# Recurrence part: the attention's output rows of both halves loaded at its beginning, into tiles that are written later

## The chip, the cores and the metric

The kernel runs on one core of one Trainium2 chip. The metric is the device time of one execution in microseconds (us), median of several runs. A core has a tensor engine for matmuls (PE, with PEld for its weight loads), a vector engine (DVE), a scalar engine (ACT), GpSimd (POOL) and a sync engine (SP); here SP only issues transfers between HBM and the on-chip memory (SBUF), in the order of its queue. ACT and POOL issue some as well. All transfers of a core run on the same 16 DMA engines.

## The reference, cut to what matters

One block of a hybrid model on 1024 tokens of width 1024, all in float32: a normalisation and an input projection, a recurrent branch (RWKV-7), a differential attention branch, a gated sum of both, an output projection, a mixture of 32 experts with two per token, and a gated extra embedding at the end. What matters here is the middle:

```python
o_rwkv = rwkv7_branch(p_rwkv, ...)            # [1024, 512], a scan over the tokens
o_diff = diff_attention_branch(p_diff, ...)   # [1024, 512]
mixed = (jax.nn.sigmoid(g_rwkv) * (o_rwkv @ w_branch_rwkv)
         + jax.nn.sigmoid(g_diff) * (o_diff @ w_branch_diff))
x = x + mixed @ w_out
```

## The kernel before

**Stages.** `build` emits: normalisation and input projection (`dense`, with the attention and the preparation of the recurrence, `w1`, spread among its matmuls); the recurrence `w2` with the branch projections as filler; the rest of the branch projections and the output projection with the router; the experts; the last stage. The attention writes its result to HBM, to `od` ([1024, 512]), one head at a time. The part that changes is the beginning of the recurrence part, some 700 us into the execution.

**The recurrence part.** `w2` runs over 8 chunks of 128 tokens. For each chunk `rwkv_gram` loads what `w1` has stored (tiles BK, AR, rows, rows2, LT; L360 to L367) and makes the Gram matrices `G` (PE L377 and L378 into the PSUM tile pG, then DVE L379); `rwkv_levels` loads the chunk's inverted blocks (Xd, L414), transposes them on DVE (L415) and inverts on PE (L422 to L449); `rwkv_step` and `rwkv_out` follow (L464 on). `rwkv_inv(1, ...)` inverts the blocks of chunks 4 to 7 on DVE alone: one load of 512 KB (`inv<-ld`, L390), then a copy (L396) and 30 pairs of multiply and add (L400, L402).

**The filler.** `fill` is a chain of generators. At each yield of `w2` a credit of 0.6 is added, and for every whole credit `fill` is advanced once. It begins with `branch_diff` for tokens 0 to 511 (half 0), then for tokens 512 to 1023 (half 1), then parts of `ple_proj` and of `branch` for the recurrent branch. `branch_diff` loads, for each of its four blocks of 128 tokens, the rows of `od` (256 KB, L779) into a tile `orow` with two buffers, transposes them with four PE instructions (L782, PSUM tile tpd, tag "a" with two buffers), and splits the transpose into a high part (ACT L76, odh) and a low part (DVE L77, odl), of which every matmul of the projection is made: `branch` (L755 to L769) loads eight slices of the weight (braw, split into bwh and bwl) and of the gate (bgt), makes 12 matmuls for each (L69 to L71, pbr), and DVE L766 writes the gated result to `md`.

**Tiles that play a part.** `md[i][k]` are four tiles of [128, 4, 512]: half i, output slices 4k to 4k+3. `md[1][1]` is first written by slices 4 to 7 of half 1. `K.orT[1]` is a pair of [128, 4, 512] tiles that `rwkv_out` fills from chunk 4 on (or1h by ACT L76, or1l by DVE L77). Both lie in memory that tiles of `w1` held before, so their first write waits for the last use of what lay there.

**What sets the order.** The text of the program gives each instruction a priority; a planner puts the instructions of each engine, and the transfers of SP's queue, in an order by that priority and by when its model thinks that an instruction's inputs and its memory are ready. So the order on a queue is not that of the text: the weight slices of `branch` (L755), for one, stand ahead of `ln_w` of `rwkv_setup` (L221). On the chip every queue then runs strictly in its order.

Of the kernel before, what the change touches and what calls it, by code (L numbers as in the profile page):

```python
# [22 lines left out]
F32 = mybir.dt.float32  # L23
# [12 lines left out]
W = 512  # L36
# [16 lines left out]
class Kern:  # L53
# [717 lines left out]
                nc.gpsimd.tensor_tensor(o, o, m, op=OP.add)  # L771
            yield

    def branch_diff(self, half, pool, md):
        nc = self.nc
        oT = [pool.tile([128, 4, 512], F32R, name=f"od{z}", tag=f"od{z}", bufs=1) for z in "hl"]
        for t in range(4):
            o = self.bp.tile([128, W], F32, name="orow", tag="orow", bufs=2)
            nc.sync.dma_start(o, self.od[half * 512 + t * 128:half * 512 + (t + 1) * 128, :])  # L779
            ps = self.ps.tile([128, 4, 128], F32, name="tpd", tag="a", bufs=2)  # L780
            for i in range(4):
                nc.tensor.transpose(ps[:, i, :], o[:, i * 128:(i + 1) * 128], self.ident)  # L782
            cs = slice(t * 128, t * 128 + 128)
            self.split(oT[0][:, :, cs], oT[1][:, :, cs], ps)
            yield
        yield from self.branch(1, half, oT, md)
# [528 lines left out]
def advance(g):  # L1315

    return next(g, StopIteration) is not StopIteration
# [14 lines left out]
def build(tc, A, out, dbg=None):  # L1332
    with ExitStack() as ctx:
        K = Kern(ctx, tc, A, out, dbg)
        nc = tc.nc
# [143 lines left out]
        md = [[K.mdtile(i).rearrange("p (k n) -> p k n", k=4) for _ in range(2)] for i in range(2)]  # L1479
        ob = [K.pool("ob1", ctx=B1, side="right")]  # L1480
# [8 lines left out]
        def from_turn(c, g):  # L1489
            while turn[0] < c:  # L1490
                yield
            yield from g


        ple = K.ple_proj(ob[0])
        fill = chain(K.branch_diff(0, ob[0], md[0]), K.branch_diff(1, ob[0], md[1]), islice(ple, 7),
                     from_turn(5, K.branch(0, 0, K.orT[0], md[0])), islice(ple, 4))
        K.credit = 0
        for c in w2():
# [94 lines left out]
```

## Time and profile before

| what | value |
|---|---|
| median of 3 runs | 1890.37 us (1888.12 to 1900.04) |
| the profiled execution | 1898.87 us, its span 1896.8 us |
| mean granted TensorE clock | 0.968 of full speed |
| PE, DVE, ACT, POOL busy | 95%, 71%, 45%, 15% of the span |
| DMA, mean over the span | 222 GB/s |

The span runs from the first to the last instruction; 2.07 us of the profiled execution lie outside it. Busy time is a mean over stages with different limits, so what one wait is worth has to be read where it stands. Matmuls are pipelined, so their bars overlap: a 128x512 matmul is listed with 0.39 us, and the next begins 0.23 us later.

### The profile page before, as it was taken

The numbers are of one execution on the slowest core, as the hardware profiler recorded it, in microseconds if no ns is written. First come the engines' busy times: TensorE is split into PE (matmuls) and PEld (weight loads), VectorE is DVE, ScalarE is ACT, GpSimd is POOL, SyncE is SP. The second block draws the span as 40 slices with busy tenths as digits, with TensorE's granted clock in tenths as the row PEclk, the third lists the DMA queues.
The fourth block names the chain that finished last, engine by engine and source line by source line (L and its number), as shares of the span: only waits on it lengthen the run. The fifth ranks groups of instructions, "written<-read, shape, count | busy, mean of one in ns | idle before, by whom it ended". The sixth has DMA issues, their size and how long they took to land. (4 is left out here: it accounts for less than half of the span.)

```text
span 1896.8 us, 28591 instructions
## 1 busy us (share of the span) xinstructions
PE 1794.4 (95%) x10864; PEld 1489.1 (79%) x10864; DVE 1342.8 (71%) x2580; ACT 858.1 (45%) x1241; POOL 275.7 (15%) x209
## 2 busy tenths in 40 slices
PE   6999999999998989999998996999999999999698
PEld 6999899898776776888876885888777777777487
DVE  6455867743777947766756668898878788888773
ACT  5244444421333322122223225777677777777431
POOL 0311201000222220010303001122111111110000
PEclk9999999999997998889998997999999999999799
DMA  6432242337576567444535557999999999999641
GB/s 219 129 117 78 79 134 79 100 112 251 192 254 228 186 206 247 141 137 158 172 110 191 176 180 254 370 367 376 328 344 356 369 357 357 348 348 354 261 176 45
DMA packets 241789, 421.39 MB, mean 222 GB/s; under 512 B 38769, under 2 KB 115697, under 8 KB 240754
## 3 DMA queue, kind: packets, MB, share of 16 engines
q1 hardware_dynamic: 194546, 346.12, 53.4%
q10 hardware_dynamic: 37888, 56.64, 8.2%
q0 software_dynamic: 9216, 16.80, 2.4%
q8 instruction: 86, 1.41, 0.3%
q14 instruction: 53, 0.43, 0.1%
HBM read 346.07 MB, written 90.18 MB: 230 GB/s over the span
## 5 line engine op out<-in xcount | busy, mean ns | idle before, releaser
L77 DVE TENSOR_TENSOR ewl<-ewp,ewh 128x2048 fp32r<-128x2048 f32 x108 | 245.6, 2286 | 38.1 <-ACT ewh L76 34.8
L69 PE MATMUL pj<-whi,hh 128*128 128x256 f32 x832 | 239.7, 288 | 0.0
L70 PE MATMUL pj<-wlo,hh 128*128 128x256 f32 x832 | 239.2, 288 | 0.3 <-DVE wlo L77 0.3
L71 PE MATMUL pj<-whi,hl 128*128 128x256 f32 x832 | 237.4, 286 | 0.0
L76 ACT ACTIVATE ewh<-ewp 128x2048 fp32r<-128x2048 f32 x108 | 204.5, 1912 | 18.3 <-PE pg L1163 8.5
L77 DVE TENSOR_TENSOR ewl<-md,ewh 128x2048 fp32r<-128x2048 f32 x84 | 191.2, 2286 | 28.0 <-ACT ewh L76 26.1
L69 PEld LDWEIGHTS pj<-whi,hh 128*128 128x128 f32 x832 | 159.2, 191 | 7.2 <-issue 6.6
L70 PEld LDWEIGHTS pj<-wlo,hh 128*128 128x128 f32 x832 | 159.2, 191 | 6.5 <-issue 5.3
L76 ACT ACTIVATE ewh<-md 128x2048 fp32r<-128x2048 f32 x84 | 159.3, 1910 | 9.6 <-PE pg L1163 4.2
L71 PEld LDWEIGHTS pj<-whi,hl 128*128 128x128 f32 x832 | 159.0, 191 | 2.6 <-issue 2.3
L1073 POOL DMA_INDIRECT xg<-h2d,ids x32 | 64.4, 2012 | 409.8 <-PE ptp L1063 390.5
L69 PE MATMUL pg<-hh,whi 128*128 128x512 f32 x256 | 105.7, 413 | 0.0
L70 PE MATMUL pg<-hl,whi 128*128 128x512 f32 x256 | 104.6, 409 | 0.0
L1163 PE MATMUL pu<-ewh,exh 128*128 128x512 f32 x256 | 103.5, 404 | 0.0
L71 PE MATMUL pg<-hh,wlo 128*128 128x512 f32 x256 | 103.1, 403 | 0.0
L1163 PE MATMUL pg<-ewh,exh 128*128 128x512 f32 x256 | 102.7, 401 | 0.0
L1163 PE MATMUL pg<-ewh,exl 128*128 128x512 f32 x256 | 102.3, 400 | 0.2 <-DVE exl L77 0.2
L1163 PE MATMUL pu<-ewh,exl 128*128 128x512 f32 x256 | 101.4, 396 | 0.0
L1116 PE MATMUL pey<-ewh,eal 128*128 128x512 f32 x256 | 97.7, 401 | 2.7 <-DVE eal L77 2.7
L1116 PE MATMUL pey<-ewh,eah 128*128 128x512 f32 x256 | 97.9, 402 | 1.4 <-ACT eah L76 1.4
L76 ACT ACTIVATE whi<-wraw 128x1024 fp32r<-128x1024 f32 x42 | 44.5, 1060 | 113.9 <-DMA wraw<-in_w_in_dram 56.4
L77 DVE TENSOR_TENSOR wlo<-wraw,whi 128x1024 fp32r<-128x1024 f32 x42 | 55.0, 1309 | 41.5 <-ACT whi L76 41.4
(457 smaller groups left out, 4262.6 us busy)
## 6 DMA issues: line engine op xcount, KB each, us to landing
ewp<-in_w_down_dram SPq DMA_DIRECT2D x42, 1024.0 KB, 7.7
ewp<-in_w_gate_dram SPq DMA_DIRECT2D x33, 1024.0 KB, 7.9
ewp<-in_w_up_dram SPq DMA_DIRECT2D x33, 1024.0 KB, 8.3
md<-in_w_up_dram SPq DMA_DIRECT2D x31, 1024.0 KB, 8.7
md<-in_w_gate_dram SPq DMA_DIRECT2D x31, 1024.0 KB, 7.6
md<-in_w_down_dram SPq DMA_DIRECT2D x22, 1024.0 KB, 7.4
wraw<-in_w_in_dram SPq DMA_DIRECT2D x42, 512.0 KB, 3.9
gd<-pjev ACTq DMA_DIRECT2D x32, 256.0 KB, 4.5
```

The lines of the kernel that those rows point to most:

```text
L69: mm(ps, lh, rh, start=start, stop=False)
L70: mm(ps, lh, rl, start=False, stop=False)
L71: mm(ps, ll, rh, start=False, stop=stop)
L76: a = nc.scalar.activation(hi, src, AF.Copy)
L77: b = nc.vector.tensor_tensor(lo, src, hi.bitcast(F32), op=OP.subtract)
L1073: self.lastx = self.nc.gpsimd.indirect_dma_start(out=xg, out_offset=None, in_=self.h2d, in_offset=bass.IndirectOffsetOnAxis(ap=tid, axis=0 ...
L1116: mm(self.pey[b], a[z][:, k + i, :], hi[:, i, half(b)], start=(k + i + z == 0), stop=False)
L1163: mm(P[i], x[z][:, k0 + j, :], hi[:, j, :], start=(k0 + j + z == 0), stop=False)
```

## The change

`branch_diff` gets one more argument, a tile `rows` of [128, 4, 512], and issues the four loads of its half into it at its start, followed by a yield. `build` makes both generators, gives half 0 the tile `md[1][1]` and half 1 the tile `K.orT[1][0]` seen as float32, and advances each once ahead of `w2`, so that all eight loads stand in the program ahead of the recurrence's own. The transposes read the new tiles. The tile `orow` of `branch_diff` is gone; `ple_proj` still has one of that tag, with 256 columns in place of 512.

```diff
-    def branch_diff(self, half, pool, md):
+    def branch_diff(self, half, pool, md, rows):
+
         nc = self.nc
+        for t in range(4):
+            r = half * 512 + t * 128
+            nc.sync.dma_start(rows[:, t, :], self.od[r:r + 128, :])
+        yield
         oT = [pool.tile([128, 4, 512], F32R, name=f"od{z}", tag=f"od{z}", bufs=1) for z in "hl"]
         for t in range(4):
-            o = self.bp.tile([128, W], F32, name="orow", tag="orow", bufs=2)
-            nc.sync.dma_start(o, self.od[half * 512 + t * 128:half * 512 + (t + 1) * 128, :])
             ps = self.ps.tile([128, 4, 128], F32, name="tpd", tag="a", bufs=2)
             for i in range(4):
-                nc.tensor.transpose(ps[:, i, :], o[:, i * 128:(i + 1) * 128], self.ident)
+                nc.tensor.transpose(ps[:, i, :], rows[:, t, i * 128:(i + 1) * 128], self.ident)
...
-        fill = chain(K.branch_diff(0, ob[0], md[0]), K.branch_diff(1, ob[0], md[1]), islice(ple, 7),
+        second = K.branch_diff(1, ob[0], md[1], K.orT[1][0].bitcast(F32))
+        first = K.branch_diff(0, ob[0], md[0], md[1][1])
+        advance(first)
+        advance(second)
+        fill = chain(first, second, islice(ple, 7),
                      from_turn(5, K.branch(0, 0, K.orT[0], md[0])), islice(ple, 4))
```

## Rows read from the trace of the kernel before

**Rows 1.** Page, part 1: busy us (share of the span) and instructions of each engine
```profile
PE 1794.4 (95%) x10864; PEld 1489.1 (79%) x10864; DVE 1342.8 (71%) x2580; ACT 858.1 (45%) x1241; POOL 275.7 (15%) x209
```

**Rows 2.** Waits of PE, 690 to 1160 us: who for whom, total, times, longest
```profile
PE tpd L782 <- DMA orow<-od: 6.7, 3, 2.7
```

**Rows 3.** Timeline of PE, half 0: start, duration, instruction, idle before and its releaser
```profile
703.44 0.60 PE L782 MATMUL tpd<-ident,orow 128*128 128x128 f32 x4
704.56 0.66 PE L782 MATMUL tpd<-ident,orow 128*128 128x128 f32 x4 [0.53 <-ACT pjev L743]
707.12 0.63 PE L782 MATMUL tpd<-ident,orow 128*128 128x128 f32 x4 [1.90 <-DMA orow<-od]
710.40 1.08 PE L782 MATMUL tpd<-ident,orow 128*128 128x128 f32 x4 [2.66 <-DMA orow<-od]
712.17 0.79 PE L69 MATMUL pbr<-odh,bwh 128*128 128x512 f32 x1 [0.69 <-ACT odh L76]
723.62 0.39 PE L71 MATMUL pbr<-odh,bwl 128*128 128x512 f32 x1
725.65 0.48 PE L377 MATMUL pG<-AR,BK 64*128 64x128 f32 x2 [1.65 <-DVE G L379]
```

**Rows 4.** Timeline of DVE around the same stretch
```profile
705.54 1.29 DVE L77 TENSOR_TENSOR odl<-tpd,odh 128x512 fp32r<-128x512 f32 x2 [0.72 <-ACT odh L76]
722.85 0.20 DVE L396 COPY inv<-inv 128x31 f32<-128x31 f32 x1 [4.65 <-DMA inv<-ld]
725.04 1.01 DVE L379 TENSOR_TENSOR G<-pG,gmask 128x384 f32<-128x384 f32 x2
```

**Rows 5.** Timeline of SP's queue: transfers as issued
```profile
672.36 22.80 SPq L348 DMA_DIRECT2D ld<-LT  x8
695.26 1.34 SPq L779 DMA_DIRECT2D orow<-od  x2
704.07 0.32 SPq L779 DMA_DIRECT2D orow<-od  x1
705.26 0.58 SPq L779 DMA_DIRECT2D orow<-od  x1
705.90 0.47 SPq L221 DMA_DIRECT2D ln_w<-in_rwkv_ln_w_dram  x1
710.13 0.52 SPq L390 DMA_DIRECT2D inv<-ld  x1
721.46 1.68 SPq L779 DMA_DIRECT2D orow<-od  x2
```

**Rows 6.** DMA issues, 706 to 724 us: count, KB each, median us to landing
```profile
DMA packets 3236, 5.85 MB, mean 325 GB/s; under 512 B 1283, under 2 KB 1795, under 8 KB 3235
inv<-ld SPq DMA_DIRECT2D x1, 512.0 KB, 12.6
ln_w<-in_rwkv_ln_w_dram SPq DMA_DIRECT2D x1, 256.0 KB, 6.2
```

**Rows 7.** Stretches: busy us by engine, PEclk, DMA share, GB/s
```profile
690.00:695.00 5.00, 5.00 (x28) 3.87 (x27) 1.29 (x2) 0.60 (x1) 0.00 (x0) 1.00 0.26 70
700.00:705.00 5.00, 4.47 (x24) 3.54 (x22) 1.46 (x3) 1.83 (x4) 2.34 (x4) 1.00 0.76 245
710.00:715.00 5.00, 3.91 (x10) 2.71 (x11) 0.69 (x1) 0.60 (x1) 0.00 (x0) 0.50 1.01 383
860.00:900.00 40.00, 40.00 (x453) 34.36 (x453) 26.15 (x65) 10.77 (x24) 2.56 (x2) 0.97 0.48 159
```

**Rows 8.** Half 1: timeline of PE, then of DVE
```profile
754.83 0.63 PE L782 MATMUL tpd<-ident,orow 128*128 128x128 f32 x4 [2.15 <-DMA orow<-od]
...
753.89 0.68 DVE L77 TENSOR_TENSOR odl<-tpd,odh 128x512 fp32r<-128x512 f32 x1
754.49 0.67 DVE L449 COPY XT<-pQ 64x512 f32<-64x512 f32 x1
```

**Rows 9.** First later writes to the second new tile
```profile
L76 ACT ACTIVATE or1h<-tpo x4: 590/597/597, 918.3 to 991.7; 128x512 fp32r<-128x512 f32 x4
```

## The prediction

> **What bounds the kernel now.** I read the page first: PE is busy for 95% of the span [rows 1], so a transfer matters only where PE stands still for it. The waits of PE from the beginning of the recurrence on come next: one row names the transfers that the change moves, 6.7 us in three waits, the longest 2.7 [rows 2]. That is all that the change aims at: 0.35% of 1898.87 us. The timelines then show where these waits stand and what would stop PE if they were gone.
>
> Half 0: the first two blocks of rows are in time. The third transpose waits 1.90 us and the fourth 2.66 us for their rows; then a split, and the first projection matmul starts at 712.17 [rows 3]. The cause is the two buffers of `orow`: the third and fourth loads go out only at 704.07 and 705.26, once transposes have freed a buffer [rows 5]. Half 1: the third transpose waits 2.15 us, until 754.83 [rows 8].
>
> The reader should also see the next gap. PE starts its last projection matmul at 723.62, stands still, and goes on at 725.65 with pG, said to wait for DVE's G [rows 3]. DVE is late because it is stuck on the copy at 722.85, which waited 4.65 us for the transfer `inv<-ld` [rows 4]. That transfer was issued at 710.13 [rows 5] and took 12.6 us to land, against 6.2 us for `ln_w`, issued at 705.90 on the same queue [rows 5, 6]. From 710 to 715 us the DMA engines are fully busy (share 1.01) [rows 7]. So this stretch is held by the DMA queue as a whole: a backlog that ends with `inv<-ld`.
>
> **The change, part by part.**
>
> *The waits of half 0.* With all rows there, what holds the third transpose is its PSUM buffer, free when the first low part is made. DVE makes two of them from 705.54 in 1.29 us [rows 4], so the first ends near 706.2 and the second near 706.8. The third transpose can start at 706.2 in place of 707.12, the fourth at 706.9 in place of 710.40. From the fourth transpose to the first matmul the trace takes 712.17 - 710.40 = 1.77 us, part of it at the low clock; I take 1.3 to 1.77, which gives 708.2 to 708.7. The projection starts 3.5 to 4.0 us earlier; I take 4.0.
>
> *What catches it.* The block from 712.17 to 725.65 then ends near 719.6 and PE again needs G. G comes after DVE's copy, and the copy after `inv<-ld`. So the gain in half 0 is not 4.0 us but what `inv<-ld` gains, unless that is more than 4.0. Everything turns on where the eight loads stand on SP's queue.
>
> *Placing A, ahead of the last `ld<-LT`.* The queue has eight of these, from 672.36 to 695.16 [rows 5], most of it waiting, and the DMA engines have room there: share 0.26 from 690 to 695 us [rows 7]. The old `orow` lies in memory that late steps of `w1` still use. The new tiles lie further to the edge of the region, by the order of allocation over tiles that the last preparations read first (their input rows). I think it likelier than not that the planner finds them free early. Then nothing of `od` is left in the crowded stretch: two issues of 0.32 and 0.58 us ahead of `ln_w` are gone [rows 5], and 2 x 0.26 = 0.52 MB at 325 GB/s (the mean of 706 to 724 us [rows 6]) are 1.6 us. `inv<-ld` lands 1.6 us (the bytes alone) to 2.5 us (both) earlier; I take 2.2. G, and PE with it, goes on at 723.45 in place of 725.65.
>
> *Placing B, behind the last `ld<-LT`,* where `orow` stands now (695.26). Then half 1's four loads, 1.05 MB, come ahead of the recurrence's loads: 1.05 MB / 325 GB/s = 3.2 us later. Some goes into the room that the DMA engines have from 700 to 705 us (share 0.76 [rows 7], so 0.24 x 5 = 1.2 us). `inv<-ld` then lands 2.0 to 3.2 us later and PE goes on at 727.7 to 728.9. The Trainium skill's page "DMA: Bandwidth & Descriptors", section "Queues, rings and completion order", says that each DMA engine consumes the descriptors of a ring in order. By that rule loads put in front delay all that follows, which speaks against this change; the landing times growing from 6.2 to 12.6 us agree with it, and it gives the case of placing B.
>
> *Half 1.* The third transpose needs the PSUM buffer of the first, whose low part DVE makes from 753.89 in 0.68 us, to 754.57 [rows 8]. It starts at 754.83 now, so 0.26 of the 2.15 us are to be had. Behind it PE needs DVE's copy of 754.49, which ends at 755.16 [rows 8]; that does not move with the loads of `od`. I take 0.3 us, bounds 0 and 2.15.
>
> *Issues and waits.* The same eight loads of 256 KB are issued, at 0.32 to 0.84 us each ([rows 5]; a pair takes 1.34 or 1.68). I cost their issue at nothing in A, where SP waits anyway; in B eight take 8 x 0.67 = 5.4 us and hold up the weight and gate slices, `ln_w` and the gram loads behind them, and the 3.2 us of transfer time run beside that. New waits: the loads wait for their tiles' former owners, and behind them on SP stand just these transfers. The other new edges cost nothing: `or1h` is first written at 918.3 [rows 9], over 150 us after the last transpose of half 1, and slices 4 to 7 of half 1 come after all transposes of half 0. The narrower `orow` of `ple_proj` saves memory and no time.
>
> *The clock.* PE is granted 0.50, the 1.2 GHz level, from 710 to 715 us after its stalls [rows 7]. PE is busy for 3.91 us of these five, so the half clock costs at most 3.91 / 2 = 2.0 us there. In A the gap at 704 to 710 shrinks but the one ahead of 723.45 grows to 3.8 us, so I count nothing either way.
>
> *Sum,* against the profiled execution of 1898.87 us (span 1896.8 and 2.07 outside): A -2.2 - 0.3 = -2.5 us, 1896.4. That execution lies 8.5 us above the median of 1890.37, so against the median the sum gives 1887.9. Once PE is past this place it is full (40.00 of 40 us from 860 to 900 [rows 7]), so what is won or lost here is carried to the end.
>
> **The rivals.**
>
> 1. *All waits go, and the gain passes.* If the loads go out early and `inv<-ld` lands by about 718.7 us, four earlier, PE loses nothing at pG: -4.0 in half 0, up to -2.15 in half 1, and up to 2.0 of low clock; I take -6.5 us, 1883.9, with -8.2 as the end. For it: the wait row's 6.7 us. Against it: the backlog of 325 GB/s would have to lose 1.3 MB, and 0.52 MB leave it.
> 2. *The transfers are only moved forward into the crowd (B).* The wait at the transposes turns into a longer wait at pG: PE reaches it at 719.6 and stands to 727.7 or later. +2.0 to +3.2, less 0.3 to 1 for half 1 and for the 0.5 MB that no longer run behind 721.46; about +2, 1892.4. It decides if the first load of `od` is issued behind the last `ld<-LT`. Slower, yet far inside 1%.
> 3. *The planner lays out another order.* The loads' earlier times can change the order of DVE and PE queues in all of the recurrence part. Nothing in the trace gives its size; the nearest rows are single waits of 2 to 3 us [rows 2, 3], so some tens of instructions would have to move badly or well to make 19 us. It can go both ways.
>
> **How the numbers follow.** Chances: A 0.45, rival 1 0.2, B 0.25, rival 3 0.1, half of it to each side. The forecast is A's: 1888.0. A's own range is 1885.7 (-2.5 and -2.15) to 1888.8 (-1.6 alone). The range has to take in rival 1 with its bounds, -8.2, so 1882.2; B's worst, +3.2, 1893.6; and that the three runs of before spread over 12 us, so that a median can lie some 3 us to either side. That gives 1878 to 1897; only rival 3 lies outside. A measurement of this kernel can tell about 1%, 19 us, from no change. A, B and rival 1 all lie within it: 0.90; rival 3 gives 0.05 to faster and 0.05 to slower.
>
> **What would show it.** Right: the row of PE waiting for `od` is gone or below 1 us; the first projection matmul of half 0 starts about 4 us sooner after the last input projection matmul; the wait at pG behind it is longer than 1.65 us; the third transpose of half 1 follows DVE's low part. A against B: on SP's queue the loads of `od` stand ahead of or behind the last `ld<-LT`, and `inv<-ld` lands earlier or later, counted from the last input projection matmul. Wrong: `inv<-ld` lands over 4 us earlier (rival 1), an `od` load holds SP for long on its tile's former owner, or the order of DVE's instructions after it is another (rival 3).

## The result, and the profile after

The changed kernel takes 1909.58 us in the median (1907.83 to 1914.94), the kernel before 1891.53 (1887.31 to 1900.04) beside it: 1.0095 times as long, 95% interval 1.0075 to 1.0115, some 18 us slower. The forecast was 1888.0 us with a range to 1897. The profiled execution of after took 1913.6 us, span 1911.5.

**Where the 18 us are.** Most of them not where the change was made. The last input projection matmul ends the part in front (703.2 us before, 701.9 after), the last transpose `tpo` the recurrence: 991.0 and 989.5, so the part that was edited takes 287.8 and 287.6 us in these two executions (others of the same two orders, further on, took 282.1 and 290.5). The difference of these two comes 450 us later, in the experts. One row for each kernel shows it; it gives the first and the last start of the transposes of the experts' inputs (tile view, PE's transposes of `xg`: count, shortest/median/longest ns, first to last start). Before, then after:

```profile
L1063 PE MATMUL ptp<-ident,xg x256: 270/272/475, 1161.2 to 1736.7; 128*128 128x128 f32 x128
```
```profile
L1066 PE MATMUL ptp<-ident,xg x256: 270/272/474, 1158.8 to 1749.7; 128*128 128x128 f32 x128
```

The same 256 transposes of the same length are spread over 575.5 us before and 590.9 after: 2.4 us ahead at the first, 13.0 behind at the last. What fills the stage shows in one stretch of it (window view, 1180 to 1730 us: length, then busy us of PE, weight loads, DVE, ACT and POOL with counts, granted clock, DMA share, GB/s), before and then after:

```profile
1180.00:1730.00 550.00, 534.51 (x2472) 426.78 (x2470) 465.85 (x353) 408.74 (x348) 97.29 (x57) 1.00 0.99 356
```
```profile
1180.00:1730.00 550.00, 528.47 (x2405) 421.75 (x2404) 455.48 (x346) 395.27 (x338) 98.56 (x56) 0.99 0.97 347
```

Before, the experts are bound by their weights: DMA share 0.99. After, the DMA engines have gaps (0.94 and 336 GB/s from 1450 us on), although not a byte and not a transfer was added here. The lower rate is the whole difference: by an estimate from these rows, 575.5 x 356 / 347 is 590 us. The waits of PE in that stretch name other instructions (who for whom: total us, times, longest). After:

```profile
PE pg L1166 <- ACT ewh L76: 9.2, 7, 2.0
PE pey L1119 <- ACT eah L76: 6.3, 9, 1.6
PE pey L1119 <- DVE eal L77: 4.7, 4, 1.6
```

Before, this was 17 short waits of `pg` for VectorE's low halves of the weights, and 2.7 and 0.7 us at `pey`; the row of the first:

```profile
PE pg L1165 <- DVE ewl L77: 11.6, 17, 0.8
```

After, PE waits longer, and for ScalarE. The rhythm tells why. ScalarE's silu `eac` comes once in each expert (timeline of ACT, lines of `eac` alone), before and then after:

```profile
1456.83 0.60 ACT L1198 ACTIVATE eac<-pg 128x512 f32<-128x512 f32 x1 [0.38 <-PE pg L1165]
1475.94 0.60 ACT L1198 ACTIVATE eac<-pg 128x512 f32<-128x512 f32 x1 [0.38 <-PE pg L1165]
1495.06 0.60 ACT L1198 ACTIVATE eac<-pg 128x512 f32<-128x512 f32 x1 [0.37 <-PE pg L1165]
1514.18 0.60 ACT L1198 ACTIVATE eac<-pg 128x512 f32<-128x512 f32 x1 [0.39 <-PE pg L1165]
```
```profile
1475.13 0.61 ACT L1201 ACTIVATE eac<-pg 128x512 f32<-128x512 f32 x1
1498.39 0.61 ACT L1201 ACTIVATE eac<-pg 128x512 f32<-128x512 f32 x1
1513.32 0.60 ACT L1201 ACTIVATE eac<-pg 128x512 f32<-128x512 f32 x1 [2.84 <-PE pg L1168]
1537.56 0.60 ACT L1201 ACTIVATE eac<-pg 128x512 f32<-128x512 f32 x1 [0.34 <-PE pg L1168]
```

Before, an expert takes 19.1 us, one like the other. After, 23.3, 14.9, 24.2. The programs show the same without any time: ScalarE's order in five experts in a row, the 14th to 18th (w a split of weights, x of inputs, a of activations, y the scaling of an output, S the silu):

```
before: wxwawxwwyywS wxwawwxwyywS wxwawwxwyywS wxwawwxwyywS wxwawwxwyywS
after:  wwaxwS wwywyxwaxwwyyxwS wwwaxwwyyxwS wxwawwwwxyywS wwaxwwwwyyxwS
```

The planner reaches one repeated pattern before and never settles after. In the expert stage the orders of ScalarE, VectorE and PE differ, SP's and GpSimd's don't. No line of the experts is in the diff.

**The edited place after.** SP's queue (timeline of SP) shows placing B; compare [rows 5]:

```profile
671.01 22.81 SPq L348 DMA_DIRECT2D ld<-LT  x8
696.67 1.77 SPq L779 DMA_DIRECT2D md<-od  x4
698.49 2.19 SPq L779 DMA_DIRECT2D or1h<-od  x4
700.72 0.43 SPq L755 DMA_DIRECT2D braw<-in_w_branch_diff_dram  x1
702.63 0.38 SPq L755 DMA_DIRECT2D braw<-in_w_branch_diff_dram  x1
703.60 0.93 SPq L1243 DMA_DIRECT2D orow<-in_p_dram  x2
709.69 0.46 SPq L221 DMA_DIRECT2D ln_w<-in_rwkv_ln_w_dram  x1
713.42 0.61 SPq L390 DMA_DIRECT2D inv<-ld  x1
```

All eight loads stand behind the last `ld<-LT` and in front of everything else; the first waited 2.5 us, released by these transfers. PE and VectorE in half 0 (timelines; compare [rows 3, 4]):

```profile
702.93 0.66 PE L785 MATMUL tpd<-ident,md 128*128 128x128 f32 x4 [0.25 <-ACT pjev L743]
709.92 1.97 PE L785 MATMUL tpd<-ident,md 128*128 128x128 f32 x8 [6.33 <-DVE odl L77]
712.58 0.79 PE L69 MATMUL pbr<-odh,bwh 128*128 128x512 f32 x1 [0.69 <-ACT odh L76]
...
706.91 0.69 DVE L77 TENSOR_TENSOR bwl<-braw,bwh 128x512 fp32r<-128x512 f32 x1 [15.60 <-ACT bwh L76]
708.50 0.69 DVE L77 TENSOR_TENSOR bwl<-braw,bwh 128x512 fp32r<-128x512 f32 x1 [0.90 <-ACT bwh L76]
709.18 1.28 DVE L77 TENSOR_TENSOR odl<-tpd,odh 128x512 fp32r<-128x512 f32 x2
```

The rows are there, and PE waits 6.33 us all the same: the third transpose needs the PSUM buffer that VectorE's `odl` frees, and VectorE stands at `bwl`, which is in front of `odl` on its queue in both kernels. `bwl` needs the first weight slices. These were issued at 696.69 before, behind two loads of rows, and are at 700.72 now, behind eight. The wait for transfers has become a wait for an engine that waits for transfers, and the projection starts 10.7 us after the last input projection matmul (9.0 before).

### The profile page after: what moved, and what is told of

It is laid out like the page before. It is cut to its first block, busy times and chain, and to the rows that moved or that the text cites. A ratio compares the mean times of both kernels' runs of the same rounds, so it can differ in the third digit from the quotient of the medians.

```text
span 1911.5 us, 28572 instructions
## 1 busy us (share of the span) xinstructions
PE 1796.7 (94%) x10864; PEld 1490.6 (78%) x10864; DVE 1347.0 (70%) x2580; ACT 856.3 (45%) x1241; POOL 278.2 (15%) x209
## 5 line engine op out<-in xcount | busy, mean ns | idle before, releaser
L1076 POOL DMA_INDIRECT xg<-h2d,ids x32 | 58.2, 1819 | 462.9 <-PE ptp L1066 443.3
L1166 PE MATMUL pg<-ewh,exh 128*128 128x512 f32 x256 | 107.0, 418 | 9.2 <-ACT ewh L76 9.2
```

Source lines behind the costliest of these rows:

```text
L1076: self.lastx = self.nc.gpsimd.indirect_dma_start(out=xg, out_offset=None, in_=self.h2d, in_offset=bass.IndirectOffsetOnAxis(ap=tid, axis=0 ...
L1166: mm(P[i], x[z][:, k0 + j, :], hi[:, j, :], start=(k0 + j + z == 0), stop=False)
```

## The experiments

All times are medians, ratios against the kernel before on the same chip. An order is held by edges between each instruction and the next on its engine; they fix the order in the engine's queue and add no wait on the chip. In the recurrence and the experts all programs here have the same compute instructions in the same sequence as recorded (e11 and e12: plus some), so one program's order can be given to another.

```diff
+        i0 = len(nc.cur_bb.bb.instructions)
         K.experts(raws, between)
...
+        pin_order(tc, nc.cur_bb.bb.instructions[i0:])
         K.overflow_loop()
...
+def pin_order(tc, ins):
...
+    for steps in json.loads(zlib.decompress(base64.b85decode(ORDER))):
...
+            tc.add_manual_dep(ins[at], ins[prev].name,
+                              mybir.DependencyInfo(C.NoSync, mybir.DependencyReason.DATA), reason="order")
```

**e1 and e2: the order in the expert stage, exchanged.** e1 is the change with the order of before there, e2 the kernel before with the order of after.

> The changed kernel, with the order of ACT's, DVE's and PE's instructions in the expert stage held to that of the kernel before; the early loads stay. Theory O (the planner's other order in the expert stage costs the time): the expert stage, first to last transpose of gathered rows, falls from 590.8 to about 575.4 us; the whole is 1889 us, 0.998 of before (the changed kernel began its experts 2.4 us earlier than before), range 1884 to 1894. Theory L (the early loads or their tiles cost it by themselves): stays near 1909 us, 1.009 of before.

> The kernel before, with the order of ACT's, DVE's and PE's instructions in the expert stage held to that of the changed kernel; its loads as before. Theory O: the expert stage rises from 575.4 to about 590.8 us, the whole to 1907 us, 1.008 of before, range 1902 to 1912. Theory L: no change, 1891 us.

e1: 1897.08 us, 1.0025 (1.0004 to 1.0046). e2: 1905.37, 1.0060 (1.0042 to 1.0079). Their expert stages take 575.3 and 587.4 us; the DMA share from 1180 to 1730 is 0.99 in e1, 0.96 in e2:

```profile
1180.00:1730.00 550.00, 533.77 (x2470) 426.29 (x2469) 466.04 (x355) 408.89 (x348) 97.25 (x57) 1.00 0.99 356
```
```profile
1180.00:1730.00 550.00, 528.29 (x2415) 421.10 (x2415) 456.52 (x346) 396.93 (x339) 99.61 (x57) 0.99 0.96 348
```

So the order of the experts, and none of the loads, makes 0.95% - 0.25% = 0.70% (13 us) by e1 and 0.60% (11 us) by e2. About 5 us (0.25%) stay in e1, more than expected.

**e3 and e4: one half alone.** In e3 half 0 is loaded early and half 1 the old way; in e4 the other way round. The edit of e3, against the change (without a tile `branch_diff` loads as before):

```diff
-        second = K.branch_diff(1, ob[0], md[1], K.orT[1][0].bitcast(F32))
+        second = K.branch_diff(1, ob[0], md[1])
         first = K.branch_diff(0, ob[0], md[0], md[1][1])
         advance(first)
-        advance(second)
```

> Half 0's four loads early into md[1][1], half 1's as before. The planner gives ACT the same order in the expert stage as before. Theory O: 1890 us, 1.000 of before, range 1885 to 1895, expert stage 575 us. Theory L: about half of the loss or more, 1900 us, since half of the loads are moved.

> Half 1's four loads early into or1h, half 0's as before. The planner's order in the expert stage falls into the steady pattern of the kernel before only at about the eighteenth expert, where before it does at the thirteenth and in the changed kernel at none. Theory O: between the two, the expert stage about 580 us, the whole 1896 us, 1.003 of before, range 1890 to 1902. Theory L: as with half 0, 1900 us.

e3: 1887.05, 0.9965 (0.9939 to 0.9991). e4: 1892.58, 1.0001 (0.9975 to 1.0026). Each came out 3 us better than its first number. With one half early, the planner finds the steady pattern (in e3 as early as before, in e4 some five experts later), and the stage takes 577.3 and 577.7 us. The loss of the experts needs both halves early. e3 lies below before with its whole interval; its profile, of the slowest of its ten executions, does not show why.

**e5 and e6: the 5 us of e1, by the queue or by VectorE.** Both hold the order of before in the experts. e5 takes both early calls away, so that half 0's loads stay where they are (the chain begins with them) and half 1's come when its turn comes; e6 keeps all loads and holds the first weight slices' splits behind the splits of the transposed rows.

```diff
-        advance(first)
-        advance(second)
```
```diff
-            self.split(wh, wl, raw)
+            self.split(wh, wl, raw, after=last if j == 0 and half == 0 else None)
```

> The changed kernel with the order of the kernel before held in the expert stage, as in e1; half 1's four loads are issued when the chain reaches half 1 and not at the beginning, half 0's four at the beginning as in the change. On SP's queue half 1's loads then stand behind the first two weight slices and gate slices, still ahead of the loads of p, of ln_w and of the recurrence's loads. Open are about 5 us that e1 (1897.1) keeps against the kernel before (1891.9) and that e3 (1887.1), with half 1 loaded the old way behind the recurrence's loads, does not show. Theory V (VectorE: the weight slices come late behind eight loads of rows, VectorE's split of them stands ahead of its split of the transposed rows, and PE waits 6.3 us for that): the weights are early again, the third transpose waits under 3 us for VectorE, the time is 1892 (1888 to 1894). Theory C (crowd: 1 MB more stands ahead of the recurrence's loads, and PE stops later at pG): nothing of that is changed, 1897 (1895 to 1900), and PE's wait at pG grows by what the transposes no longer wait. If the 5 us are neither, both kernels of V come out within 2 us of e1.

> The changed kernel with the order of the kernel before held in the expert stage, as in e1, and the queue order of all eight loads as in the change; in half 0 the splits of the first weight slices are held behind the splits of all four transposed blocks, on ScalarE and VectorE. Theory V (PE's 6.3 us at the third transpose come from VectorE standing at the weight slices' split): the wait of the transposes for VectorE falls to under 1.5 us, the first projection matmul starts under 9 us after the last input projection matmul (10.7 in the change), and the time is 1892 (1888 to 1894). Theory C (1 MB more ahead of the recurrence's loads): the transposes go early too, but what they win is lost again at pG, where the wait grows from 0.9 to 3 us and more; 1896 to 1898.

e5: 1900.65, 1.0049 (1.0031 to 1.0067). e6: 1883.87, 0.9954 (0.9938 to 0.9971), 9 us faster than before. Neither theory survives: both times lie outside the ranges of both. In e5 the wait for VectorE at the transposes fell from 6.3 to 2.2 us and the kernel got no faster; in e6 it fell to 3.4 only, on the queue order of the change, and the kernel got 13 us faster than e1. e6's edge had made the planner lay out the whole recurrence anew: it puts the gram matmuls and the projection side by side, and its recurrence takes 275.7 us (e1 290.5, e5 291.5). The window view of the whole recurrence, from the last input projection matmul to the last `tpo`, for before, after and e6:

```profile
703.20:991.00 287.80, 274.58 (x2481) 227.76 (x2480) 187.27 (x445) 65.17 (x131) 32.61 (x25) 0.92 0.51 160
```
```profile
701.90:989.50 287.60, 270.83 (x2482) 225.08 (x2480) 188.63 (x446) 65.82 (x132) 33.05 (x25) 0.93 0.51 162
```
```profile
701.00:976.70 275.70, 262.39 (x2481) 216.68 (x2480) 186.57 (x445) 65.73 (x132) 32.89 (x25) 0.96 0.53 169
```

PE stands still for 13.2, 16.8 and 13.3 us (length less busy), which does not tell e6 from before; the busy time differs by 12 us for the same matmuls, and the column that goes with it is the granted clock, 0.92, 0.93 and 0.96. I cut the recurrence of each kernel into stretches of 5 us and summed the idle time and, for the clock, busy time times one less the granted clock:

| kernel | recurrence | PE idle | lost by the clock | rest |
|---|---|---|---|---|
| before | 287.8 | 13.2 | 20.2 | 254.4 |
| before's recurrence in e2 | 282.1 | 12.4 | 14.9 | 254.8 |
| after | 287.6 | 16.8 | 16.0 | 254.8 |
| the same code in e1 | 290.5 | 15.7 | 19.6 | 255.2 |
| e3 | 284.8 | 13.9 | 15.7 | 255.2 |
| e4 | 282.4 | 13.4 | 14.0 | 255.0 |
| e5 | 291.5 | 15.2 | 20.4 | 255.9 |
| e6 | 275.7 | 13.3 | 8.2 | 254.2 |

The rest is the work at full clock, 254 to 256 us in all of them. The idle time moves by 4 us; what the clock takes moves by 12. The same code shows 20.2 and 14.9 in two executions (the change's 16.0 and 19.6), so that one profile of this stage says little to within 5 us. The idle time scatters less: 13.2 and 12.4 us for the code of before, 16.8 and 15.7 for the change's, 2.5 to 4.4 us more with the early loads.

**e7: ScalarE's order alone.** As e1, but with only ScalarE's order held.

> The changed kernel with the order of the kernel before held in the expert stage for ScalarE's instructions alone; VectorE's and PE's are laid out by the planner around it. If ScalarE's order (when the splits of the next weights stand ahead of or behind the splits of activations) is what costs the 12 to 13 us of the expert stage: time 1897 (1894 to 1900), expert stage about 576 us, PE waits for the weights' low halves in 17 waits again. If VectorE's or PE's order decides: 1903 to 1910, expert stage 583 to 591 us.

1930.00, 1.0201 (1.0172 to 1.0230), expert stage 609.1 us: outside both numbers, and worse than either whole order. ScalarE then has the order of before to the letter, and the planner's new order of VectorE and PE around it does not fit: PE waits 17.9 us for `ewh` at `pu`. Which engine's order costs can't be said one engine at a time.

**e8: no loads at all.** The transposes read the constant mask, so the rows' share of the result is missing; the order of before is held in the experts.

```diff
-            nc.sync.dma_start(rows[:, t, :], self.od[r:r + 128, :])
...
-                nc.tensor.transpose(ps[:, i, :], rows[:, t, i * 128:(i + 1) * 128], self.ident)
+                nc.tensor.transpose(ps[:, i, :], self.mask[:, i * 128:(i + 1) * 128], self.ident)
```

> The changed kernel with the order of the kernel before held in the expert stage, and without the eight loads of the attention's output rows: the transposes read a constant tile that is there from the start, so the attention's branch is left out of the result. This gives what no placement of these loads can beat. The prediction's first rival (all waits go and the gain passes on) has 6.5 us less than the kernel before: 1885 (1882 to 1888). If PE is stopped again at pG by the recurrence's own loads, whatever the rows do: the 1 MB of half 0 that is gone brings them at most 3 us forward, so 1888 to 1891, and a wait at pG of 2 us or more. If the recurrence takes up neither: 1892.

1958.45 us, but that total says nothing: with other values the router spreads the tokens otherwise, and a block of the overflow loop runs that the other kernels don't need (264 transposes of `xg` in place of 256). The recurrence lies in front of that. It takes 277.8 us, PE idle for 10.6, 14.9 lost by the clock. So without any of these loads the idle time is 13.2 - 10.6 = 2.6 us shorter than before (1.8 against e2's), about what the prediction's sum had (2.5), in an order of the recurrence that was not held. PE is stopped at `pG` all the same, now by the recurrence's own load, which is the expectation's second case (timeline of PE, the projection beginning at 710.60):

```profile
714.64 0.81 PE L377 MATMUL pG<-AR,BK 64*128 64x128 f32 x4 [3.46 <-DMA AR<-spAR]
```

**e9 and e10: layout against loads.** Now the orders of PE, ScalarE and VectorE are held from the recurrence to the experts' end: e9 is the kernel before with e6's order, e10 the change with the order of before.

> The kernel before, with its late loads into two buffers, and the order of PE's, ScalarE's and VectorE's instructions that the planner gave e6, from the recurrence's beginning to the end of the experts; SP's and GpSimd's orders are the planner's. In its profile e6 needs 275.7 us from the last input projection matmul to the end of the recurrence, the kernel before 287.8, the change 287.6. If the layout of the recurrence is what makes e6 fast and not its loads: 1884 (1880 to 1887), recurrence 274 to 279 us. If the early loads and the earlier splits make it: 1892 (1889 to 1895), recurrence 282 to 288 us, as the kernel before.

> The change with the order of PE's, ScalarE's and VectorE's instructions of the kernel before in the recurrence too, not only in the expert stage as in e1 (1897.1): what is left of the change is the loads. If the loads cost nothing and the 5 us of e1 are the layout of the recurrence: 1892 (1889 to 1895). If the loads themselves cost it (1 MB more ahead of the recurrence's loads, weight slices late): 1897 (1895 to 1900). If they bring what the prediction said, with the layout out of the way: 1889 or less.

e9: 1887.74, 0.9969 (0.9953 to 0.9985), between its two ranges; its recurrence takes 278.3 us, within the first, with 15.2 idle and 8.7 lost by the clock. With the late loads of before, two thirds of e6's gain (0.31 of 0.46%) come from the order alone; whether e6's loads make the rest is not settled, as the intervals overlap. e10: 1895.87, 1.0009 (0.9987 to 1.0032), which is from 2.5 us faster to 6.1 slower. By the time alone, the loads can't be told from nothing. The profile (of an execution of 1902.92 us, above the median) shows what they do in the order of before. PE waits 7.3 us for VectorE's `odl` at the third transpose. VectorE's copy of `inv` comes 24.3 us after the last input projection matmul (at 701.6), 19.7 before, and PE, waiting for the G behind it, goes on with `pG` 27.5 us after that matmul, 22.4 before (timelines of PE and DVE; compare [rows 3, 4]):

```profile
729.07 0.79 PE L377 MATMUL pG<-AR,BK 64*128 64x128 f32 x2 [3.13 <-DVE G L379]
725.92 0.20 DVE L396 COPY inv<-inv 128x31 f32<-128x31 f32 x1 [5.78 <-DMA inv<-ld]
```

Its recurrence takes 295.7 us: 17.0 idle (13.2 and 12.4 with the late loads), 24.4 lost by the clock, rest 254.3. So the loads hold PE up by some 4 us; how much of that reaches the time is not settled.

**e11: is a short stall paid twice?** The kernel before with 14 more matmuls at a place where PE stands still for 1.2 us; they repeat what was just written to their buffer.

```diff
+            if (c, h) == (2, 6):
+                for _ in range(7):
+                    self.again += [
+                        nc.tensor.matmul(ps[:, 0, :], BK[o:o + 64, pr, 0, :], AR[o:o + 64, pr, 1, :], start=True, stop=True),
+                        nc.tensor.matmul(ps[:, 1:3, :], BK[o:o + 64, pr, 1, :], AR[o:o + 64, pr, :, :], start=True, stop=True)]
...
+            if name == "PE" and n == 435:
+                order += again
```

> The kernel before with every engine's order as it is and 14 matmuls more: two of the gram matmuls of one head are repeated seven times, into the same buffer with the same values, right ahead of the place where PE stands still for 1.2 us about 93 us after the last input projection matmul (795 us in the profile of before). In that profile the granted clock is 0.72 to 0.85 in the 40 us from 80 to 120 us behind that matmul, 8.6 us lost by the clock, and 1.00 behind it. If a short stall is paid twice, once as itself and once by the clock that falls after it: PE is busy in that place, the clock stays at 1.00, and more work takes less time, 1885 to 1889. If the clock falls there for another reason: 1892 to 1893.

1886.22, 0.9962 (0.9942 to 0.9982): 7 us less for more work. The stall in the timeline of before, and the 80 us from 80 us behind the last input projection matmul on (window view), before and then e11:

```profile
795.97 0.48 PE L377 MATMUL pG<-AR,BK 64*128 64x128 f32 x2 [1.21 <-DVE G L379]
...
783.20:803.20 20.00, 18.80 (x210) 16.74 (x210) 12.27 (x25) 2.29 (x6) 1.30 (x2) 0.85 0.46 142
803.20:823.20 20.00, 20.00 (x102) 16.55 (x102) 10.29 (x28) 4.25 (x8) 2.55 (x2) 0.72 0.44 144
823.20:843.20 20.00, 20.00 (x248) 17.71 (x247) 12.79 (x33) 3.77 (x9) 0.00 (x0) 1.00 0.39 124
843.20:863.20 20.00, 19.02 (x124) 14.39 (x123) 11.83 (x25) 4.26 (x9) 2.55 (x2) 0.74 0.50 143
```
```profile
780.80:800.80 20.00, 20.00 (x238) 17.79 (x237) 12.36 (x24) 2.18 (x5) 2.04 (x2) 1.00 0.41 122
800.80:820.80 20.00, 20.00 (x168) 16.64 (x168) 14.62 (x33) 4.87 (x10) 2.58 (x2) 1.00 0.60 197
820.80:840.80 20.00, 19.81 (x219) 16.85 (x217) 13.71 (x37) 5.03 (x11) 2.55 (x2) 1.00 0.50 152
840.80:860.80 20.00, 19.89 (x217) 16.26 (x218) 13.67 (x28) 3.85 (x8) 0.00 (x0) 1.00 0.48 144
```

In before, a stall of 1.2 us is followed by a stretch at the 1.2 GHz level: 0.15 x 18.8 + 0.28 x 20 = 8.4 us lost, which at 0.50 are 17 us of low clock. One of 0.9 us at 849 costs 0.26 x 19 = 4.9 us more. In e11 PE is busy through the first, the clock stays at 1.00, and the second is down to 0.2 us, with no low clock behind it.

The first place is alike in e2's execution of the same order (timeline, and the 20 us from the stall on):

```profile
793.35 0.48 PE L377 MATMUL pG<-AR,BK 64*128 64x128 f32 x2 [1.00 <-DVE G L379]
793.30:813.30 20.00, 19.95 (x148) 17.59 (x149) 8.90 (x26) 3.29 (x7) 2.54 (x2) 0.57 0.38 122
```

The second is not: in e2 it lasts 0.4 us and the clock stays at 1.00, so only the first can be put down to the added matmuls. The kernel before with its order held and nothing added was not run, but e10, held in the same order, still has the low clock there (window view, 20 us from 100 us behind the last input projection matmul on):

```profile
801.60:821.60 20.00, 18.90 (x143) 16.81 (x144) 8.84 (x27) 2.83 (x7) 2.54 (x2) 0.57 0.38 122
```

Not every such stall is followed by a low clock. One of 1.39 us in e6, at 752, is not, nor one of 1.13 us in e4 (timeline, and the 20 us from there on); what sets them apart is open:

```profile
847.43 0.49 PE L70 MATMUL ppp<-odl,bwh 128*128 128x512 f32 x1 [1.13 <-DVE odl L77]
847.40:867.40 20.00, 19.87 (x217) 16.25 (x218) 13.67 (x28) 3.84 (x8) 0.00 (x0) 1.00 0.46 143
```

e11's recurrence is 278.0 us: idle 11.5, lost by the clock 7.6, rest 259.0, which is 4.6 more than before for the added matmuls, all of them paid.

The Trainium skill's page "TensorE: Matmul & The Clock Gate", section "A second HAM failure mode: psum-queue depth-cycling", tells of a kernel whose frequent brief idle times between groups of matmuls, while PSUM buffers are cycled, make the clock swing between its levels. The trace agrees in part: this stall is of that kind (PE waits for VectorE to free the PSUM buffer pG), and a single one of 1.2 us was enough. The two above that no low clock followed wait for data that VectorE makes, but so does the one at 849 that one did follow.

**e12: both together.** e6 with its own orders held and three such pairs ahead of its stall of 1.7 us.

> e6 (1883.9) with every engine's order as it is and six matmuls more: two gram matmuls of one head repeated three times into the same buffer, right ahead of PE's stall of 1.7 us about 71 us after the last input projection matmul, which is followed by a granted clock of 0.73 and 0.96 in e6's profile (2.7 and 0.8 us lost). In e11 such a pair took 0.66 us, so three are 2.0 us. If the stall is paid twice as e11 showed: the clock stays at 1.00 there and the time is 1880 (1877 to 1882). If e6 was fast for another reason and this place does not matter: 1884 to 1885.

1888.49, 0.9969 (0.9949 to 0.9989): outside both numbers and no better than e6 (0.9954). In its profile the clock behind the place is 1.00 as wanted, 3.3 us less are lost by it (4.9 against 8.2) and 0.7 less in idle time, but the work at full clock grew by 3.0. That nets 1 us, and its executions spread more (1880.9 to 1896.7) than e6's (1880.7 to 1888.5). The filling is worth it where much clock is lost behind a stall, as in before; here little was.

## Why the prediction was wrong, step by step

**Placing A failed, as the likeliest case.** "I think it likelier than not that the planner finds them free early" was an argument from the order of allocation with no row behind it. The queue shows B: issue at 696.67, behind the last `ld<-LT`, and its first load waited for that transfer.

**B's own sum was right in kind and too small.** `inv<-ld` is issued 11.5 us after the last input projection matmul, 6.9 before: 4.6 later, where 2.0 to 3.2 stood; two loads of p came in front too, and the third and fourth weight slices were issued later. It landed 12.7 us after its issue (12.6 in [rows 6]). PE pays for it at another place than the prediction's. In the change one G (720.15) stands ahead of VectorE's copy of `inv`, so that `pG` and `pR` run at 724.6 and 725.4 without a wait; the next two stand behind the copy, and PE waits for them, 2.34 and 0.92 us (0.55 and 0.91 in e1's execution of this order, where `inv<-ld` kept VectorE for 3.7 us in place of 5.5). Timelines of PE, then of DVE:

```profile
728.17 0.69 PE L422 MATMUL pQ<-Xd,LT 32*32 32x32 f32 x32 [2.34 <-DVE G L379]
729.78 0.68 PE L377 MATMUL pG<-AR,BK 64*128 64x128 f32 x2 [0.92 <-DVE G L379]
...
726.24 0.19 DVE L396 COPY inv<-inv 128x31 f32<-128x31 f32 x1 [5.53 <-DMA inv<-ld]
727.51 0.56 DVE L379 TENSOR_TENSOR G<-pG,gmask 128x384 f32<-128x384 f32 x1
```

In e10, in the order of before, PE goes on at `pG` itself, 5.0 us later. So the second rival, at 0.25, is what the traces show in half 0; its "+2" is 2.5 to 4.4 us more idle time in the change and e1.

**The third transpose "can start at 706.2"** counted VectorE's `odl` by its time of before. Removing a wait for a transfer put eight loads ahead of the weight slices, and VectorE's next instruction needed these. It started 8.0 us after the last input projection matmul, not 3.0.

**Half 1's term** (0.3 us) had the right reason: the 2.15 us of waiting for the transfer became 0.58 for VectorE's `md` and, behind it, 1.46 for VectorE's copy XT, 0.1 less in all. Two slips of the sum change nothing: the block of half 0 ends 0.4 us after the start of its last matmul, which was taken for its end, and 1882.2 less 3 is 1879, not 1878.

**The clock: "I count nothing either way".** The runs do not refute this for the change: 20.2 and 14.9 us are lost in two executions of the order of before, 16.0 and 19.6 in two of the change's. But the term is no small one. It scatters by 4 to 5 us in the same order, and in e6's it is 8.2, 12 less than in before's profile, more than all the waits that [rows 2] names.

**"What is won or lost here is carried to the end"** failed most of all; it put everything behind the edited place at nothing. It was read from PE being full at 860 us [rows 7], and holds up to 1160 in the profiles shown. Behind that comes a stage whose order the planner makes anew for each program, and that order alone costs 13 us by e1 and 11 by e2, while the edited place moved the time by some 5 us (e1). The third rival had the mechanism, the planner's order, but placed it "in all of the recurrence part" and gave it 0.05 on this side; the moves that cost most stand in another stage, and the row that would have warned of it is the DMA share of 0.99 there, which leaves no room for a worse order.

**The sum of the 0.95%:** 0.6 to 0.7% are the experts' order (e1, e2: shown). What e1 keeps, 0.25%, is 0.09% in e10, when the recurrence's order is held too. By the times, the share of that order (some 3 us) and of the loads (some 2) can't be told from each other or from nothing, as the intervals overlap; by PE's idle time, the loads cost some us in both orders. Why the planner settles in a pattern with either half early and in none with both is left open: what it assumes at the experts' beginning was not looked at.

## What to carry to other kernels

Where a planner orders instructions, compare the order of the stages that were not edited before explaining a time, and hold the order in one kernel of the comparison: a small edit here slowed a DMA-bound stage 450 us away by 11 to 13 us, nearly twice all the waits that it was to remove (6.7). Before removing a wait, read what stands in front of the releasing instruction on its engine, and what the moved transfers now stand in front of. In a stage full of matmuls with short stalls, sum idle time and clock apart.

## What the hardware showed unexpectedly

A short PE stall can cost more by the clock behind it than by itself: 1.2 us idle and 8.4 us lost at 1.2 GHz in before, alike in e2, and 14 superfluous matmuls (4.6 us) in its place went with a kernel 7 us faster. It is no rule: stalls of 1.13 us (e4) and 1.39 us (e6) cost no more than themselves. The clock's part also makes most of the scatter between executions of one order in this stage: 287.8 and 282.1 us, with 20.2 and 14.9 us lost.
